# Softmax attention on one core: the second pair of heads taken in halves, one late group shared by two engines, and the order of the work read from a table

## The chip, the core and the metric

The kernel runs on one core of a Trainium2 chip. Five engines work side by side, each through its own list of instructions in order: TensorE (PE) multiplies matrices, VectorE (DVE) and ScalarE (ACT) work element by element, GpSimd (POOL) converts types here, and SyncE (SP) issues most of the transfers. They wait for each other by semaphores. The metric is the time of one execution on the device, in microseconds (us); below, a time without a unit is in us from the start of the profiled span.

## The reference

```python
def reference(q, k, v):                      # each 8 x 8 x 512 x 64, float32
    scale = 1.0 / np.sqrt(q.shape[-1])
    scores = np.einsum('bhqd,bhkd->bhqk', q, k) * scale
    scores = scores - scores.max(axis=-1, keepdims=True)
    attn = np.exp(scores)
    attn = attn / attn.sum(axis=-1, keepdims=True)
    return np.einsum('bhqk,bhkd->bhqd', attn, v).astype(np.float32)
```

That is 64 independent heads, each with 512 queries and 512 keys of 64 numbers, and 512 x 512 exponentials per head. The kernel leaves the subtraction of the maximum out and uses one constant shift instead; the division by the sum takes it out again.

## The kernel before

Two heads, a and b, make a *pair*; there are 32 pairs, 0 to 31. The 512 keys of a head are cut into 4 chunks of 128. The scores of one chunk of one head (128 keys by 512 queries) are a *block*, written a0 to a3 and b0 to b3, and two blocks are a *group*: one PSUM tile `st` of 128 x 1024 float32. There are 128 groups, `m` = 0 to 127; the last is worked in two halves of 256 queries, numbered 127 and 128. Three `st` tiles exist, so the scores of group m use the tile that group m-3 held.

What each pair goes through:

- **Load** (SP, `load`): k, q and v, 256 KB each, seven buffers of each.
- **Round to fp16** (`cast`): POOL writes k and q into `qkp` and v into `vp`. For pair 1, VectorE rounds half of q (line 523) and POOL the other half (line 524).
- **Turn** (PE, `transposes`, line 558): 8 transposes per pair into a PSUM bank `tp`; VectorE copies the result to `tqk` (line 571; for pair 1 in two copies, first k and then q of both heads, line 565). In `tqk` head a lies on partitions 0 to 63 and head b on 64 to 127.
- **Scores** (PE, line 598): two matmuls of 64 x 128 by 64 x 512 per group.
- **Exponential**: ScalarE makes one ACTIVATE of a whole group (line 602) into `pt`. 16 of the groups (`ON_DVE`) go to VectorE instead: `raise_` (line 625) reads the scores out of PSUM, which frees the `st` tile, and five passes (lines 642 to 665) make two fp16 factors, `pe` and `pd`, whose values are both fed to PE.
- **Values** (PE, line 704): for each head 4 *units* of 128 queries; each is 4 matmuls, and one more for every block that VectorE made. Seven units share a PSUM bank `o`. When a bank is full, VectorE takes the reciprocals of the sums (`rec`, line 671) and multiplies (`mul`, line 676) into a ring buffer, from which SP stores. `tp` and `o` share two banks, so a new `o` waits for the `mul` two banks before it.
- **The last head** has code of its own: `last_values` in four parts, the last two after the halves 127 and 128, and then `finish`: reciprocal, multiply, store.

The order of all this is written by `Plan`, a planner that steps through time with built-in costs (lines 18 to 425) and returns a list of steps; each step then records instructions on its engine. The order is fixed: an engine that waits holds back what is listed after it. Pair 0 is worked by its own code, `first_pair`, and its last group (m = 3) is the first that the planner's steps give to ScalarE.

Of the kernel before, what the change touches and what calls it, by code (L numbers as in the profile page):

```python
# [17 lines left out]
class Plan:  # L18

    SLOT, EXP, EXP_DONE, EXP_FIXED = 216, 853, 181, 64  # L20
    INTO, OUT_OF = 96, 96
    TRANSPOSE, V_UNIT = 222, 128
    TO_ACT, TO_DVE, TO_PE = 220, 210, 60

    COPY, NORM, RAISE = (601, 690), (50, 133), (1132, 1215)
    RECIPROCAL = 115
    SCALE, PRODUCT, EXTRA = 333, 600, 29
    COPY_1 = (400, 190)
    NORM_COLUMN, PASS_DONE = 67, 115
    PASSES = (SCALE, SCALE, PRODUCT, SCALE, PRODUCT)  # L30
    BITS = 2
    NEEDS = (None, None, 0, 2, 3)
    FIRST_EXP = 5000
    STEP = 5
    CALM, KEEN = 9000, 4
    FIRST_UNIT = 4
    KNOWN, OVER = (13, 15, 18, 20, 22, 24, 27, 42, 50, 61, 69, 97), 6
    ON_DVE = (5, 10, 16, 25, 28, 39, 44, 54, 63, 66, 74, 81, 91, 96, 103, 116)

    LATE_NORM, LATE_COPY, HURRY, SOON, BACKLOG = 700, 1500, 800, 160, 600  # L40
    LATE_MUL, WAIT = 400, 200
    SLACK, AHEAD = 0, 2

    CAST, CAST_PORT, CAST_DONE, TO_POOL = 557, 475, 130, 150
    SCALE_PORT, PRODUCT_PORT, GAP, REACH = 271, 537, 20, 5
    FIRST_LAND, LOAD, STORE, LATENCY, ISSUE = 5200, 752, 376, 2300, 470
    QUEUED, URGENT = 3500, 16
    PAIRED, STORE_ISSUE = 18, 520
    RAW, QK16, NV, NU = 7, 5, 12, 112
    PAIR, DUEK, DUEV, DUEL, PRE = 3300, 3550, 6000, 5000, 0  # L50

    def __init__(self, groups, pairs, first):
        self.groups, self.pairs = groups, pairs
        self.pe, self.act, self.dve = 7000, self.FIRST_EXP, 6300
        self.pool, self.port, self.dma = 4600, 4600, self.FIRST_LAND
        self.m, self.tiled = first, True
        self.read = []
        self.exps = {}
        for m in range(first):
            self.act += self.EXP + self.EXP_FIXED  # L60
            self.exps[m] = self.act + self.EXP_DONE
            self.read.append(self.exps[m])
        self.tq = {0: 5800}
        self.transposed = {0: 5800}
        self.next_t = 1
        self.part_t = 0
        self.banks = [5100, 5800]
        self.todo = [(g, h) for g in range(pairs) for h in range(2)]
        self.last = self.todo.pop()
        self.last_part = 0  # L70
        self.head = None
        self.units = self.FIRST_UNIT
        self.member = {b: m for m, grp in enumerate(groups) for b in grp}
        self.ready = []
        self.passes = []
        self.passed = {}
        self.raised = set()
        self.steps = []
        self.busy_dve = 0
        self.order, self.paired = [], 0  # L80

        late = {grp[0][0] for m, grp in enumerate(groups) if m in self.ON_DVE}
        due = []
        for g in range(pairs):
            scores = 5000 + self.PAIR * g
            if g:
                due += [(scores - self.DUEK, g, "k"), (scores - self.DUEK + 10, g, "q")]
            due.append((scores + self.DUEV + (self.DUEL if g in late else 0), g, "v"))
        self.due = sorted(due)
        self.uncast = list(self.due)  # L90
        self.casts = []
        self.landed, self.cast_done = {}, {}
        self.first_loads = [(g, n) for _, g, n in self.due if g < self.RAW]
        self.first_loads += [(self.RAW, "k"), (self.RAW, "q")]
        for x in self.first_loads:
            self.dma += self.LOAD
            self.landed[x] = self.dma
        self.loads, self.stores, self.stored = [], [], []
        self.sp = 1650 + 470 * len(self.first_loads)

    def note(self, t, *what):
        self.steps.append((t, len(self.steps)) + what)

    def trigger(self, t):

        ops = self.ops
        if not ops or ops[-1][1] <= t - 300:  # L110
            return 1, None
        n = len(ops) - 1
        while (
            n > 0
            and len(ops) - n < self.REACH
            and not ops[n][2]
            and ops[n][0] - ops[n - 1][1] <= self.GAP
        ):
            n -= 1
        if n > 0 and ops[n][0] - ops[n - 1][1] <= self.GAP:  # L120
            n -= 1
        return len(ops) - n, ops[n][1]

    def emit(self, t, back, after):
        _, g, n = self.uncast.pop(0)
        shared = (g, n) == (1, "q")
        self.note(t, "cast", g, n, back if t > self.CALM else 0)
        if not shared:
            self.casts.append((g, n, t if after is None else after + self.TO_POOL))
# [3 lines left out]
    def fits(self, t, soon=0):  # L133
        if not self.uncast:
            return False
# [763 lines left out]
```

## Time and profile before

| | us |
|---|---|
| median of 3 runs (113.44 to 113.83) | 113.63 |
| the profiled execution, whole | 113.92 |
| its span, first to last instruction | 112.1 |
| ScalarE busy in the span | 105.5 |
| TensorE busy | 103.2 |
| VectorE busy | 100.8 |
| GpSimd busy | 65.9 |

The profile is of one execution. The terms of a sum are differences inside that execution; it took 0.29 more than the median, and that offset, like the 1.8 outside the span, is carried along unchanged. In the rows, a line such as "9.21 1.02 ACT L602 ACTIVATE pt<-st" says: starts at 9.21, lasts 1.02, on ScalarE, from line 602, writes `pt` and reads `st`; in brackets stand the engine's idle time before it and what ended it. Where "x5" ends a row, five instructions in a row are merged, and the duration runs from the first start to the last end.

### The profile page before, as it was taken

The page shows a single profiled execution, that of the slowest core. Times are in us where ns is not written, and L with a number is a line of the kernel's source. Part 1 is how long each engine was busy: PE and PEld are TensorE (multiplying, and loading weights), DVE is VectorE, ACT ScalarE, POOL GpSimd, SP SyncE. Part 2 cuts the span into 40 slices and gives each one's busy share as a digit, 9 for nine tenths or more (in the row PEclk, how much of TensorE's full clock was granted, in tenths as well). Part 3 has the DMA queues.
Part 4 walks back from the last instruction along what each step waited for, and adds up shares of the span by engine and source line. Part 5 has one row for each costly group of instructions (what it writes and reads, how often), then busy time and mean ns, then how long its engine had stood idle before and what let it go on. Part 6 is the DMA issues. An engine that isn't in the chain of part 4 may idle for free.

```text
span 112.1 us, 4408 instructions
## 1 busy us (share of the span) xinstructions
PE 103.2 (92%) x1728; PEld 69.4 (62%) x1728; DVE 100.8 (90%) x227; ACT 105.5 (94%) x118; POOL 65.9 (59%) x127
## 2 busy tenths in 40 slices
PE   7978889999799998999989999899999999999980
PEld 7634555766367766658647767577557577675660
DVE  1647999999999999999999999999999999997390
ACT  4599999999999999999999999999999999999970
POOL 2147768549756886495594786876784855600000
PEclk9999999999999999999999999999999999999997
DMA  3999999999999999999999999999999974142354
GB/s 106 276 359 353 345 350 347 355 336 349 345 347 336 341 346 343 354 364 375 370 358 382 350 355 377 354 372 362 343 366 305 349 245 143 52 141 99 97 167 161
DMA packets 35093, 33.84 MB, mean 302 GB/s; under 512 B 2304, under 2 KB 35072, under 8 KB 35072
## 3 DMA queue, kind: packets, MB, share of 16 engines
q1 hardware_dynamic: 34496, 33.04, 90.4%
q10 hardware_dynamic: 576, 0.52, 1.4%
q8 instruction: 13, 0.21, 0.8%
q14 instruction: 8, 0.07, 0.2%
HBM read 25.17 MB, written 8.39 MB: 299 GB/s over the span
## 4 chain that ended last, share of the span: by engine, by line
DVE 39%; PE 24%; DMA 15%; issue 8%; POOL 7%; SPq 3%; ACT 2%; POOLq 0%; ACTq 0%
PE o L704 13%; DMA v<-in_v_dram 10%; PE st L598 8%; DVE pd L625 8%; DVE tqk L571 7%; DVE ring L676 7%; DMA q<-in_q_dram 5%; DVE m L659 4%; POOL qkp L525 4%; DVE pd L665 4%; POOL vp L515 3%; PE tp L558 2%; SPq L509 2%; DVE m L642 2%; DVE pe L651 2%
## 5 line engine op out<-in xcount | busy, mean ns | idle before, releaser
L602 ACT ACTIVATE pt<-st 128x1024 f16<-128x1024 f32 (+1 forms) x110 | 100.3, 1144 | 0.2 <-PE st L598 0.2
L704 PEld LDWEIGHTS <-pt 128*128 128x128 f16 x880 | 38.8, 98 | 12.1 <-issue 10.2
L704 PE MATMUL o<-vp,pt 128*128 128x65 f16 x880 | 45.3, 194 | 0.4 <-POOL vp L515 0.2
L598 PE MATMUL st<-tqk 64*128 64x512 f16 (+1 forms) x250 | 41.7, 380 | 2.6 <-ACT pt L602 1.4
L525 POOL CAST qkp<-k 128x512 f16<-128x512 f32 x31 | 22.2, 717 | 11.3 <-DVE rc L671 5.3
L525 POOL CAST qkp<-q 128x512 f16<-128x512 f32 x30 | 21.7, 725 | 9.0 <-DVE rc L671 5.3
L515 POOL CAST vp<-v 128x512 f16<-128x512 f32 x32 | 21.4, 679 | 9.2 <-PE st L598 2.4
L676 DVE TENSOR_TENSOR ring<-o,rc 128x448 f32<-128x448 f32 (+2 forms) x37 | 22.3, 606 | 0.4
L704 PE MATMUL o<-vp,pe 128*128 128x65 f16 x128 | 21.8, 194 | 0.0
L704 PE MATMUL o<-vp,pd 128*128 128x65 f16 x128 | 21.7, 192 | 0.0
L558 PE MATMUL tp<-ident,qkp 128*128 128x128 f16 x248 | 19.6, 220 | 1.6 <-DVE tqk L571 0.8
L558 PEld LDWEIGHTS <-qkp 128*128 128x128 f16 x248 | 14.4, 97 | 9.9 <-issue 4.6
L571 DVE COPY tqk<-tp 128x1024 f16<-128x1024 f16 x30 | 20.3, 683 | 0.0
L625 DVE TENSOR_SCALAR pd<-st 128x1024 uint16<-128x1024 f32 x16 | 19.5, 1216 | 0.7 <-PE st L598 0.7
L598 PEld LDWEIGHTS <-tqk 64*128 64x128 f16 x250 | 10.7, 93 | 11.8 <-issue 4.6
L704 PEld LDWEIGHTS <-pe 128*128 128x128 f16 x128 | 12.5, 98 | 3.4 <-issue 3.3
L704 PEld LDWEIGHTS <-pd 128*128 128x128 f16 x128 | 12.5, 98 | 0.0
L659 DVE TENSOR_TENSOR m<-m 128x1024 f16<-128x1024 f16 x16 | 11.0, 685 | 0.0
L665 DVE TENSOR_TENSOR pd<-pd,m 128x1024 f16<-128x1024 f16 x16 | 10.9, 684 | 0.0
L671 DVE RECIPROCAL rc<-o 128x7 f32<-128x7 f32 (+2 forms) x37 | 7.4, 199 | 2.6 <-PE o L704 2.4
L661 DVE TENSOR_SCALAR m<-m 128x1024 f16<-128x1024 f16 x16 | 6.7, 418 | 0.1
L651 DVE TENSOR_SCALAR pe<-pd 128x1024 uint16<-128x1024 uint16 x16 | 6.6, 411 | 0.0
(51 smaller groups left out, 34.9 us busy)
## 6 DMA issues: line engine op xcount, KB each, us to landing
v<-in_v_dram SPq DMA_DIRECT2D x32, 256.0 KB, 5.8
k<-in_k_dram SPq DMA_DIRECT2D x31, 256.0 KB, 5.8
q<-in_q_dram SPq DMA_DIRECT2D x31, 256.0 KB, 5.9
out_dram<-ring SPq DMA_DIRECT2D x18, 256.0 KB, 5.5
out_dram<-ring SPq DMA_DIRECT2D x25, 128.0 KB, 2.2
k<-in_k_dram ACTq DMA_DIRECT2D x2, 128.0 KB, 2.8
q<-in_q_dram SPq DMA_DIRECT2D x2, 128.0 KB, 2.6
out_dram<-ring ACTq DMA_DIRECT2D x2, 128.0 KB, 1.9
```

Of the source, the lines that this page charges most:

```text
L515: return nc.gpsimd.tensor_copy(out=vps[g % NV][:, :, :, 0:D], in_=raw[g]["v"][:, :, :, :])
L525: return nc.gpsimd.tensor_copy(out=dst, in_=src[:, :, :, :])
L558: reads[g] = nc.tensor.transpose(tps[g][:, n, i, :], qkp[g][:, n, i, :], ident)
L571: nc.vector.tensor_copy(out=tqk[g][:, :, :], in_=tps.pop(g).rearrange("p n i c -> p n (i c)"))
L598: nc.tensor.matmul(st[:, x, cols], kc, qc[:, cols], start=True, stop=True)
L602: ins = nc.scalar.activation(out=pt[:, :, cols], in_=st[:, :, cols], func=EXP, scale=scale, bias=SHIFT)
L625: nc.vector.tensor_scalar(out=r["pd"][:, :, :], in0=r["st"][:, :, :], scalar1=BITS, scalar2=BIAS, op0=AluOp.mult, op1=AluOp.add,)
L651: ins = nc.vector.tensor_scalar(out=r["pe"][:, :, :], in0=u[:, :, :], scalar1=0x7C00, scalar2=None, op0=AluOp.bitwise_and,)
L659: ins = nc.vector.tensor_tensor(out=m16, in0=m16, in1=m16, op=AluOp.mult)
L665: ins = nc.vector.tensor_tensor(out=u16, in0=u16, in1=m16, op=AluOp.mult)
L676: nc.vector.tensor_tensor(out=ring[:, u % NU : u % NU + n, :], in0=o[:, x : x + n, 0:D], in1=rcs.pop(u)[:, 0:n].broadcast_to([P, n, D]), o ...
L704: nc.tensor.matmul(os[u // 7][:, u % 7, :], part[:, y * P : (y + 1) * P], vps[g % NV][:, h, c, :], start=(n == 0), stop=(n == len(parts) - 1),
```

## The change

Five things change; the arithmetic of the result does not.

1. **The order** is no longer planned: `Order` holds it as text, one letter per step (S scores, T transposes, V a unit of values, K a cast, C a copy, R a raise, N and M a bank's reciprocals and multiply, and so on). Counts of every kind of step stay what they were, apart from pair 1. The groups on VectorE are again 16, but other ones.
2. **Pair 1** is loaded as four transfers of 128 KB (k and q of head a, then of head b) instead of two of 256 KB, rounded head by head (k on POOL, q on VectorE), turned head by head and copied head by head. Its groups are a0a1, a2b0, a3b1, b2b3 where they were a0b0, a1b1, a2b2, a3b3, so the first needs head a alone.
3. **The last pair**: a0b0, a1b1, a2a3, b2b3 where it was a0a1, a2a3, b0b1, b2b3.
4. **Group 120**, the last of the 16, is shared: ScalarE takes its first block, VectorE raises the second alone. Before, the last of the 16 was group 116, wholly on VectorE.
5. A cast's dependence on VectorE is counted along one list, `trail`; the fp16 tiles of a raised group are taken at the raise.

```diff
+class Order:
+
+    ON_DVE = (5, 11, 15, 26, 31, 38, 47, 55, 59, 71, 81, 84, 96, 103, 108, 120)
+    SPLIT = (120,)
+    PAIR_1 = "a0a1 a2b0 a3b1 b2b3"
+    LAST_PAIR = "a0b0 a1b1 a2a3 b2b3"
...
+        "KSDKTDCTKSCKSSRKTTSKCVVVaSNScVSKMTdTbSCKVVRKSVTKSeTSCVKSfKRSTGKTVSKCVSkTNgSKMTSCKVVhSGVV"
...
+            if g == 1 and name in "kq":
+                halves.append((load_tile(g, name), source(src, g)))
+                if len(halves) == 2:
+                    for h in range(2):
+                        for t, rows in halves:
+                            nc.sync.dma_start(out=t[:, h], in_=rows[:, h])
+                continue
...
-        if (g, name) == (1, "q"):
-            nc.vector.tensor_copy(out=dst[:, :, 0:2], in_=src[:, :, 0:2])
-            return nc.gpsimd.tensor_copy(out=dst[:, :, 2:4], in_=src[:, :, 2:4])
+        dst, src = rounded(g, name), raw[g][name]
+        if g == 1:
+            h = "kq".index(name)
+            return nc.gpsimd.tensor_copy(out=rounded(1, "k")[:, h], in_=raw[1]["k"][:, h])
...
+    def cast_queries(h):
+        dve(nc.vector.tensor_copy(out=rounded(1, "q")[:, h], in_=raw[1]["q"][:, h]))
...
+    def head_transposes(h, bank):
+
+
+        cols = slice(0, 64 + 64 * h)
+        t = ps_x.tile([P, 2, NI, P], FP16, tag=f"x{bank ^ h}", name=f"tp_1_{h}")
+        for n in (1, 0):
+            for i in range(NI):
+                reads[1] = nc.tensor.transpose(t[cols, n, i, :], qkp[1][:, n, i, cols], ident)
+        flips.append(t)
...
+            h = len(copied)
+            rows = slice(64 * h, 64 * h + 64)
+            copied.append(
+                dve(
+                    nc.vector.tensor_copy(
+                        out=tqk[1][rows, :, :], in_=flips[h][rows].rearrange("p n i c -> p n (i c)")
+                    )
+                )
+            )
...
+        own = 0 if on_dve and m not in Order.SPLIT else 1 if on_dve else 2
...
+            if x < own:
+                blocks[(g, c, h)] = [pt[:, x, :]]
+        if own == 0:
             return
         ins = nc.scalar.activation(
-            out=pt[:, :, cols], in_=st[:, :, cols], func=EXP, scale=scale, bias=SHIFT
-        )
...
+            out=pt[:, 0:own, cols], in_=st[:, 0:own, cols], func=EXP, scale=scale, bias=SHIFT
+        )
...
-                out=r["pd"][:, :, :],
-                in0=r["st"][:, :, :],
+                out=r["pd"][:, own:2, :],
+                in0=r["st"][:, own:2, :],
```

**VectorE at pair 1, before.** Its list from the end of pair 0 on (`qkp` are the rounded k and q, `tqk` the turned ones, `tp_1_0` the turned k and `tp_1_1` the turned q, `pd_5` the first raise):

```order
L835 COPY qt_0_169<-tp_qb_180 128x256 [waits PE_49]
L523 CAST qkp_1_275<-q32_1_110 128x2x2x64 [waits DMAHW5_49]
L565 COPY tqk_1_284<-tp_1_0_285 128x512 [waits PE_49]
L565 COPY tqk_1_284<-tp_1_1_293 128x512 [waits PE_49]
L625 TENSOR_SCALAR pd_5_307<-st_5_305 128x1024 [waits PE_49]
L571 COPY tqk_2_317<-tp_2_0_318 128x1024 [waits PE_49]
```

**The same place after.** Here `tp_1_0` and `tp_1_1` are head a and head b:

```order
L563 COPY qt_0_171<-tp_qb_182 128x256 [waits PE_49]
L241 CAST qkp_1_277<-q32_1_109 128x4x64 [waits DMAHW5_49]
L241 CAST qkp_1_277<-q32_1_109 128x4x64 [waits DMAHW7_49]
L281 COPY tqk_1_286<-tp_1_0_287 64x1024 [waits PE_49]
L281 COPY tqk_1_286<-tp_1_1_298 64x1024 [waits PE_49]
L350 TENSOR_SCALAR pd_5_325<-st_5_316 128x1024 [waits PE_49]
L288 COPY tqk_2_328<-tp_2_329 128x1024 [waits PE_49]
```

Both casts of q stand ahead of both copies, and the second waits for the fourth transfer.

**VectorE at the last raise, before.** `rc` and `ring` are the reciprocals and the multiply of a bank of units (the numbers behind `rc` count units), `m` the passes' working tile:

```order
L671 RECIPROCAL rc_210_2696<-o_30_2649 128x7 [waits PE_49]
L676 TENSOR_TENSOR ring_85<-o_30_2649,rc_210_2696 128x448 [waits DMAHW6_49,DVE_49]
L625 TENSOR_SCALAR pd_116_2701<-st_116_2699 128x1024 [waits PE_49]
L571 COPY tqk_31_2721<-tp_31_0_2722 128x1024 [waits PE_49]
L642 TENSOR_SCALAR m_116_2758<-pd_116_2701 128x1024 [waits DVE_49]
L651 TENSOR_SCALAR pe_116_2700<-pd_116_2701 128x1024
L659 TENSOR_TENSOR m_116_2758<-m_116_2758 128x1024 [waits DVE_49]
L671 RECIPROCAL rc_217_2793<-o_31_2685 128x7 [waits PE_49]
```

**The same place after:**

```order
L399 RECIPROCAL rc_217_2773<-o_31_2713 128x7 [waits PE_49]
L350 TENSOR_SCALAR pd_120_2782<-st_120_2761 128x512 [waits Activation_49]
L404 TENSOR_TENSOR ring_85<-o_31_2713,rc_217_2773 128x448 [waits DMAHW4_49,DVE_49]
L399 RECIPROCAL rc_224_2818<-o_32_2775 128x7 [waits PE_49]
L393 TENSOR_TENSOR pd_108_2504<-pd_108_2504,m_108_2645 128x1024
L404 TENSOR_TENSOR ring_85<-o_32_2775,rc_224_2818 128x448 [waits DMAHW5_49,DMAHW1_49,DVE_49]
L399 RECIPROCAL rc_231_2866<-o_33_2827 128x7 [waits PE_49]
L370 TENSOR_SCALAR m_120_2873<-pd_120_2782 128x512
L404 TENSOR_TENSOR ring_85<-o_33_2827,rc_231_2866 128x448 [waits DMAHW4_49,DVE_49]
```

The raise waited for PE; now it waits for ScalarE, which reads the other half of the same tile, and the multiply of bank `o_31` and the last pass of group 108 are listed behind it.

**TensorE at the scores that take the raised tile, before** (`st_119` takes the tile of group 116; the other names are values of pair 25 and scores of pair 30):

```order
L704 MATMUL o_31_2685<-vp1_87,pd_103_2396 128x65
L598 LDWEIGHTS tqk_29_2459
L598 MATMUL st_119_2753<-tqk_29_2459 128x512 [waits DVE_49]
L598 MATMUL st_119_2753<-tqk_29_2459 128x512
L598 LDWEIGHTS tqk_30_2614
L598 MATMUL st_120_2760<-tqk_30_2614 128x512 [waits Activation_49]
```

**and after** (`st_122` and `st_123` are scores of pair 30, `o_33` the next bank of values):

```order
L316 MATMUL st_122_2813<-tqk_30_2550 128x512
L316 LDWEIGHTS tqk_30_2550
L316 MATMUL st_123_2821<-tqk_30_2550 128x512 [waits DVE_49]
L316 MATMUL st_123_2821<-tqk_30_2550 128x512
L432 LDWEIGHTS pt_116_2668
L432 MATMUL o_33_2827<-vp5_91,pt_116_2668 128x65 [waits DVE_49]
```

(In both, the weight load before a tile's second matmul is left out, as it only repeats.) The scores of group 123 wait for the raise of group 120, whose tile they take, and the bank `o_33` waits for the multiply of `o_31`. Behind these stand, in this order: 20 matmuls of values of pair 29, 10 of group 108's pair (its `pd` is one of the factors), the scores of groups 124 and 125, 34 and 4 matmuls of values, the scores of 126 and 127, 28 matmuls of values (20 of them with the factors of group 120), the scores of 128, 16 of head a of the last pair, and the last head.

More of the change, by code (lines that the diff above doesn't have):

```diff
@@ L1 @@
 import math
+import re
 from contextlib import ExitStack
@@ L477 @@
     raw = {}
+    halves, flips, copied = [], [], []
     qkp = {}
@@ L866 @@
         }
-        for what, *args in steps:
+        for what, *args in order.steps():
             do[what](*args)
```

531 lines of the change are left out of this document (118 added, 413 removed), and 13 rows, old and new, of tables (CASTS, HEADS, LOADS).

## Prediction

> **What bounds the kernel now.** I read the page first, for the busy shares:
>
> ```profile
> span 112.1 us, 4408 instructions
> PE 103.2 (92%) x1728; PEld 69.4 (62%) x1728; DVE 100.8 (90%) x227; ACT 105.5 (94%) x118; POOL 65.9 (59%) x127
> ACT  4599999999999999999999999999999999999970
> ```
>
> Three engines lie within 5% of each other, so shares don't decide; what decides is which engine never waits. The chain of waits wanders (VectorE, TensorE, GpSimd, transfers), which says that most of them are just in time. ScalarE's own instructions in order of time, and then its groups by shape, settle it:
>
> ```profile
> 5.20 0.60 ACT L801 ACTIVATE pt<-st_0a 128x512 f16<-128x512 f32 x1 [0.43 <-PE st_0a L794]
> 5.69 0.59 ACT L801 ACTIVATE pt<-st_0b 128x512 f16<-128x512 f32 x1
> 6.17 1.95 ACT L801 ACTIVATE pt<-st 128x1024 f16<-128x1024 f32 x2
> 7.98 1.06 ACT L602 ACTIVATE pt<-st 128x1024 f16<-128x1024 f32 x1
> 9.21 99.28 ACT L602 ACTIVATE pt<-st 128x1024 f16<-128x1024 f32 x109 [0.18 <-PE st L598]
> ```
>
> ```profile
> L602 ACT ACTIVATE pt<-st 128x1024 f16<-128x1024 f32 x108 | 99.4, 1153 | 0.2 <-PE st L598 0.2
> L602 ACT ACTIVATE pt<-st 128x512 f16<-128x512 f32 x2 | 1.1, 616 | 0.0
> ```
>
> The exponentials overlap, so their mean of 1153 ns is no price; the distance of their ends is. The first half ends at 5.20+0.60 = 5.80 and the second at 5.69+0.59 = 6.28: 0.48 for a half. Group 4 ends at 9.21+1.02 = 10.23 (its row stands below) and the last at 9.21+99.28 = 108.49; between lie 106 whole groups and two halves, so a whole one costs (98.26 - 0.96)/106 = 0.918. Groups 1 and 2, with nothing to wait for, end together at 8.12, 1.84 after group 0: 0.92 each. So from 10.23 to 108.49 ScalarE ran at the price it has undisturbed: nothing is to be gained there unless it does fewer exponentials. Its only lost time is ahead of group 4: group 3 ended at 7.98+1.06 = 9.04, group 4 could have ended at 9.96 and ended at 10.23, 0.27 later. After the last exponential the span goes on for 3.6.
>
> The Trainium skill (ScalarE: Activation LUTs, What ACT_TABLE_LOAD costs) gives an ACTIVATE with immediate scale and bias 186 ns + 0.833 ns per element, less 93 ns of overlap: an estimate of 0.95 for a group and 0.52 for a half. The rows have 0.918 and 0.48, so the measurement decides; by the page the first term below would be 0.04 larger.
>
> How much room is there before ScalarE waits? An exponential that had to wait lasts 1.02 from start to end:
>
> ```profile
> L602 ACT ACTIVATE pt<-st x9: 1024/1057/1110, 99.1 to 106.5; 128x1024 f16<-128x1024 f32 x9
> ```
>
> One that lasts longer stood ready beside the one before it. Near the end the shortest took 1.024: that group's scores came with no room at all. A schedule that is a little later there makes ScalarE wait, with all the rest behind it.
>
> **First term: the shared group.** Both lists have 16 groups on VectorE, but the last now leaves its first block to ScalarE: one half more, **+0.48**, on the engine that sets the time. Nothing covers it. What it saves (VectorE half a raise and five half passes, PE four matmuls of values) lies on engines that ScalarE doesn't wait for.
>
> **Second term: the start.** Pair 1 before:
>
> ```profile
> 6.65 0.62 POOL L525 CAST qkp<-k 128x512 f16<-128x512 f32 x1 [2.98 <-DMA k<-in_k_dram]
> 7.32 0.94 PE L558 MATMUL tp<-ident,qkp 128*128 128x128 f16 x8 [0.44 <-POOL qkp L525]
> 7.37 0.29 DVE L523 CAST qkp<-q 128x256 f16<-128x256 f32 x1 [1.15 <-DMA q<-in_q_dram]
> 7.40 0.52 POOL L524 CAST qkp<-q 128x256 f16<-128x256 f32 x1
> 7.76 0.97 DVE L565 COPY tqk<-tp 128x512 f16<-128x512 f16 x2
> 8.78 0.82 PE L598 MATMUL st<-tqk 64*128 64x512 f16 x6 [0.52 <-DVE tqk L565]
> 9.21 1.02 ACT L602 ACTIVATE pt<-st 128x1024 f16<-128x1024 f32 x1 [0.18 <-PE st L598]
> 9.43 1.23 DVE L625 TENSOR_SCALAR pd<-st 128x1024 uint16<-128x1024 f32 x1 [0.70 <-PE st L598]
> 10.57 0.68 DVE L571 COPY tqk<-tp 128x1024 f16<-128x1024 f16 x1
> ```
>
> k lands at about 6.6 and q at 7.35, so 0.75 per 256 KB. The same bytes in four parts land at about 6.22, 6.6, 6.98 and 7.37. VectorE rounds q of head a by 6.9 (0.29), the transposes take 0.6 after it (7.66 to 8.26 before) and end at 7.5. The copy can't start then: the second cast of q stands ahead of it and ends at 7.66. The copy's 64 x 1024 isn't in the trace; its bounds are 0.42 to 0.49 (the 512-element copies) and 0.68 (1024 elements), and I take 0.68, since the rows differ by elements per partition. It ends at 8.3. Group 4 is now two blocks of one head: its matmuls use the same rows of PE and follow each other, 0.21 more than two heads, by these rows of the chain and of the timeline:
>
> ```profile
> 102.98 0.60 PE st L598 x2
> ```
>
> ```profile
> 97.60 0.39 PE L598 MATMUL st<-tqk 64*128 64x512 f16 x2
> ```
>
> From the first matmul to the exponential it was 9.21-8.78 = 0.43; so 8.33+0.43+0.21 = 8.97, 0.24 earlier: **-0.24**. At best all 0.27 come back; at worst none, if the small transfers land late. Head b's copy ends at 9.0, so the raise of group 5 stays at 9.5 (9.43 before) and pair 2's copy with it. Two more transfers on SP cost it two issues, under cover of a queue that is full. The rest of the order table I cost at nothing: steps of the same kinds and number; its cover is the room ScalarE has in front of each group.
>
> **Third term: what waits for group 120.** Prices of one step, from the chain, where each piece runs to the start of the next:
>
> ```profile
> 13.76 1.13 DVE pd L625
> 20.97 0.11 DVE rc L671
> 21.37 0.53 DVE ring L676
> 21.91 0.60 DVE pd L665
> 33.77 1.40 PE o L704 x40
> 35.17 0.54 PE st L598 x4
> ```
>
> A matmul of values is 1.40/40 = 0.035. A half raise isn't in the trace: between 0.56 (half of 1.13) and 1.13, nearer the half, and I take 0.60 with 0.69 to its own end (the multiplies of 256 and 448 elements, 0.42 and 0.62, differ by 1.0 ns per element; 1.23 less 512 of these). Let Z be the end of the half exponential of 120. Without waits the last one ends at Z + 6 x 0.918 + 0.98 = Z+6.49. VectorE reaches this raise early (what is listed ahead of it waits only for values that PE lists before the scores of 120, and these come two groups before ScalarE needs them) and is held there until Z, since it waits for ScalarE. It ends at Z+0.7; PE stands at the scores of 123 and starts them at Z+0.75. The multiply behind the raise ends at Z+1.25, so bank `o_33` starts at Z+1.3; the last pass of 108 (after a reciprocal) ends at Z+1.95 and is in time. 30 matmuls: Z+2.38, the scores of 124. They were needed by: end of exponential 123 (Z+2.75) + 0.918 - 1.02 - 0.43 = Z+2.22. **+0.16.** Scores of 124 and 125, then 38 matmuls, put the scores of 126 at Z+4.2, and 126 is of one head: its exponential starts at Z+4.85 and ends at Z+5.87; from 124 on it would have been Z+5.67. **+0.20.** The last exponential ends at Z+6.85. Bounds of this term: 0 (VectorE not held) and 0.8 (the raise at the whole price of 1.13 holds PE 0.5 longer).
>
> **Fourth term: the last steps.** Now:
>
> ```profile
> 107.49 0.68 PE L704 MATMUL o<-vp,pt 128*128 128x65 f16 x16
> 108.01 0.84 PE L720 MATMUL o_last<-vp,pt 128*128 128x65 f16 x16
> 108.43 0.42 DVE L676 TENSOR_TENSOR ring<-o,rc 128x256 f32<-128x256 f32 x1
> 108.89 0.18 DVE L733 RECIPROCAL rc_last<-o_last 128x4 f32<-128x4 f32 x1
> 109.55 0.33 SPq L740 DMA_DIRECT2D out_dram<-obl x1
> ```
>
> The last head's reciprocal starts 0.40 after the last exponential. Head a of the last pair now needs group 126 (its a2a3) instead of 125, so its 16 matmuls start about when 128's scores are done, Z+6.05, and end at Z+6.65; its reciprocal and multiply (0.22, 0.42) end at Z+7.5 and stand ahead of `rc_last`: Z+7.53 instead of 6.85+0.40 = 7.25. **+0.28**, with bounds of 0 and 0.4.
>
> **Sum:** 0.48 - 0.24 + 0.36 + 0.28 = +0.88. On the profiled 113.92 that is 114.80; on the median, 113.63, it is 114.51.
>
> **Rivals.**
>
> *The wait at group 120 is covered.* If PE gets through its values somewhat faster, or the raise isn't held, terms three and four nearly vanish: 0.48 - 0.24 = +0.24, 113.9. For it: the list keeps most of this work early enough to miss by 0.2 only. Against: shortest exponential of 1.024, no room. The Trainium skill (PSUM — Partial Sum Buffer, Specifications (TRN2)) says that ScalarE and VectorE read PSUM in parallel at full bandwidth if their banks differ; by that rule the raise could run beside the half exponential. In this list it waits for it, whatever the banks allow.
>
> *The price of ScalarE isn't a floor (faster).*
>
> ```profile
> 7.07 1.04 ACT L801 ACTIVATE pt<-st 128x1024 f16<-128x1024 f32 x1
> ```
>
>  Starts follow each other by 0.91, as group 2's and group 3's (7.98) do, where ends do by 0.918; were the difference a wait for scores, up to 0.01 x 106 = 1.1 would be left in the order, and a better table would take it out: 113.63 + 0.24 - 1.1 = 112.8. It decides from a price below 0.912 per group on. Against it: the two undisturbed groups at the start cost 0.92.
>
> *The small transfers land late.* Pair 1 gains nothing and the sum is +1.12: 114.75.
>
> *The new table makes ScalarE wait in mid-run.* 15 other groups sit on VectorE, each holding one of three tiles. If ten of them cost 0.1, +1.0: 115.5. For it: the room above. Against: the list before has it nowhere after 10.23.
>
> **How the numbers follow.** Mine 45%, covered wait 25%, late transfers 10%, waits in mid-run 12%, floor not a floor 8%. The likeliest is 114.5, its own range 114.1 to 114.9. The range reaches down to the covered case and up half way to the mid-run waits: 113.8 to 115.2. A measurement of this kernel can tell about 0.3%, 0.34, from no change: below 113.29 lies only the floor rival, 8%; within lie some two thirds of the covered case, 17%; the rest, 75%, is slower.
>
> **What would show it.** Right: group 4's exponential at about 9.0; distance of ends still 0.918 up to group 120; VectorE idle ahead of a 128x512 raise, released by ScalarE; idle time of ScalarE at the end, released by PE; the last reciprocal more than 0.4 after the last exponential. Wrong: ScalarE's groups closer than 0.912, or VectorE's raise of 120 well before the half exponential ends.

## The result, and the profile after

The changed kernel takes **115.27 us** (median of 4 runs, 115.11 to 115.47), and the kernel before, on the same chip, 113.73 (113.44 to 114.05). The ratio is **1.0136**, with a 95% interval of 1.0103 to 1.0168: slower by 1.54. The forecast was 114.5, 113.8 to 115.2.

The profiled executions are 115.25 and 113.92, their spans 113.48 and 112.10; the difference of the spans, 1.38, is what the rows below divide up. (The medians are 1.54 apart; the profiled execution of the kernel before took 0.19 more than its median.) First the busy shares of the changed kernel:

```profile
PE 106.5 (94%) x1732; PEld 70.3 (62%) x1732; DVE 102.1 (90%) x228; ACT 106.3 (94%) x119; POOL 63.0 (56%) x127
```

The shares say as little as before; PE's busy time even rose by 3.3 with four matmuls more. ScalarE's instructions in order of time say more (line 529 is pair 0, line 321 the rest):

```profile
6.13 1.95 ACT L529 ACTIVATE pt<-st 128x1024 f16<-128x1024 f32 x2
7.93 6.78 ACT L321 ACTIVATE pt<-st 128x1024 f16<-128x1024 f32 x7
14.92 94.69 ACT L321 ACTIVATE pt<-st 128x1024 f16<-128x1024 f32 x104 [0.20 <-PE st L316]
```

Before, the first group of pair 1 (group 4) was late; now its exponential follows the one before. But there are two new losses. The seven ending at 7.93+6.78 = 14.71 follow one that ended at 8.08: 6.63, where seven back to back take 7 x 0.917 = 6.42. By the single ends in the trace, 0.226 is lost ahead of group 7, the last of pair 1. And 0.311 is lost ahead of group 12, the first of pair 3, which starts at 14.92. From there on the ends are 0.917 apart again (0.915 to 0.918 for 100 of the groups), up to the end of the kernel:

```profile
104.20 1.24 ACT L321 ACTIVATE pt<-st 128x1024 f16<-128x1024 f32 x1
105.55 1.94 ACT L321 ACTIVATE pt<-st 128x1024 f16<-128x1024 f32 x2
107.61 1.51 ACT L321 ACTIVATE pt<-st 128x1024 f16<-128x1024 f32 x2
```

The first row is group 123, ending at 105.44. Groups 124 and 125 end together at 107.49, 2.05 later instead of 1.83, and 126 with the first half after it at 109.12, 1.63 later instead of 1.41: 0.22 lost ahead of 124 and 0.23 ahead of 126.

| part of the span | before | after | difference |
|---|---|---|---|
| end of the first two half exponentials | 6.28 | 6.24 | -0.04 |
| waits of ScalarE up to group 12 | 0.335 | 0.537 | +0.20 |
| small waits and rounding in between | 0.02 | 0.04 | +0.02 |
| the half exponential of group 120 | none | 0.490 | +0.49 |
| waits ahead of 124 and 126 | none | 0.446 | +0.45 |
| last exponential to the landing of the last store | 2.77 | 2.80 | +0.03 |
| that landing to the end of the span | 0.84 | 1.06 | +0.22 |
| sum | | | +1.37 |

**The start.** The rows around pairs 1 to 3 in the changed kernel:

```profile
5.08 0.38 PE L522 MATMUL st<-qt,kt 64*128 64x512 f16 x2
7.47 1.41 DVE L281 COPY tqk<-tp 64x1024 f16<-64x1024 f16 x2 [0.63 <-PE tp L272]
9.31 0.61 POOL L226 CAST qkp<-q 128x512 f16<-128x512 f32 x1
9.47 0.91 PE L263 MATMUL tp<-ident,qkp 128*128 128x128 f16 x8
10.31 0.60 PE L316 MATMUL st<-tqk 64*128 64x512 f16 x2
10.78 0.61 POOL L226 CAST qkp<-k 128x512 f16<-128x512 f32 x1
11.09 0.58 DVE L370 TENSOR_SCALAR m<-pd 128x1024 uint16<-128x1024 uint16 x1
11.53 0.61 POOL L226 CAST qkp<-q 128x512 f16<-128x512 f32 x1
11.71 0.98 DVE L387 TENSOR_TENSOR m<-m 128x1024 f16<-128x1024 f16 x1
12.61 0.34 DVE L404 TENSOR_TENSOR ring<-o,rc 128x192 f32<-128x192 f32 x1
13.10 0.61 PE L263 MATMUL tp<-ident,qkp 128*128 128x128 f16 x8 [0.61 <-DVE ring L404]
13.74 0.69 DVE L288 COPY tqk<-tp 128x1024 f16<-128x1024 f16 x1
```

The four halves land at 5.42, 5.76, 6.14 and 6.51, far earlier than I had put them (6.22 to 7.37), and the copies of pair 1 start at 7.47 (7.76 before). But pair 2's k and q land at 8.54 and 9.26, against 8.09 and 8.85. The cast of q (9.31) and with it the transposes (9.47 to 10.38) are late, and the scores of group 7, which need neither, stand behind those transposes: 10.31. From the landing of that q to the end of group 7's exponential it takes 2.715 here, and 2.718 and 2.715 in the two other executions of the new table in which group 7 waited (experiments 3 and 9): the landing sets this wait.

Pair 3 is late for another reason. Its copy (13.74) follows its transposes (13.10), and these need a bank that the multiply of the first units (line 404) frees; that multiply now stands behind the product pass of line 387, at 12.61. And this pass took 0.98, beside the cast of pair 3's q on GpSimd (11.53 to 12.14), as the pass of line 370 took 0.58 beside that of k; with no cast beside them these passes take 0.69 and 0.42 (experiments 5 and 10). In the kernel before:

```profile
10.72 0.62 POOL L525 CAST qkp<-k 128x512 f16<-128x512 f32 x1 [0.46 <-DVE pd L625]
11.56 0.72 POOL L525 CAST qkp<-q 128x512 f16<-128x512 f32 x1 [0.23 <-DVE rc L671]
11.73 0.35 DVE L676 TENSOR_TENSOR ring<-o,rc 128x192 f32<-128x192 f32 x1
12.49 0.67 DVE L659 TENSOR_TENSOR m<-m 128x1024 f16<-128x1024 f16 x1
13.09 0.68 DVE L571 COPY tqk<-tp 128x1024 f16<-128x1024 f16 x1
```

There both casts of pair 3 waited for VectorE, the product pass took 0.67, and one other pass was held up beside a cast (line 651, 0.57). In the new table (`3k 3q`, without a number) they wait for their loads alone, and start 0.05 after these land. From the copy of pair 2 to that of pair 3 it took 2.52 before, with three passes between, and 3.24 now, with four.

**The end.** Around the raise of group 120:

```profile
102.72 0.69 DVE L350 TENSOR_SCALAR pd<-st 128x512 uint16<-128x512 f32 x1 [0.93 <-ACT pt L321]
103.33 0.61 DVE L404 TENSOR_TENSOR ring<-o,rc 128x448 f32<-128x448 f32 x1
103.47 0.39 PE L316 MATMUL st<-tqk 64*128 64x512 f16 x2 [0.29 <-DVE pd L350]
103.99 0.80 PE L432 MATMUL o<-vp,pt 128*128 128x65 f16 x20
105.06 0.61 PE L316 MATMUL st<-tqk 64*128 64x512 f16 x4
106.91 0.60 PE L316 MATMUL st<-tqk 64*128 64x512 f16 x4
109.48 0.18 DVE L399 RECIPROCAL rc<-o 128x4 f32<-128x4 f32 x1
109.70 0.42 DVE L404 TENSOR_TENSOR ring<-o,rc 128x256 f32<-128x256 f32 x1
110.04 0.17 DVE L461 RECIPROCAL rc_last<-o_last 128x4 f32<-128x4 f32 x1
```

VectorE stood 0.93 for ScalarE with the raise at its head; PE then waited for the raise (103.47) and for the multiply behind it (103.99), and the scores of 124 and 126 came at 105.06 and 106.91.

**After the last landing.** Instructions of SyncE at the kernel's last line, from the last store's landing on, in the kernel before and then in the changed one (last line 894 and 622; the window opens at 111.26 and at 112.41):

```profile
L894 SPq EVENT_SEMAPHORE  x2: 17/22/28, 111.3 to 111.6; - x2
```

```profile
L622 SPq EVENT_SEMAPHORE  x6: 17/28/1305, 111.1 to 112.9; - x6
```

SyncE checks the transfers' semaphores one after the other. In the changed kernel it stood in one of these checks for 1.3 when the store landed, and four more came after, at 112.467, 112.531, 112.593 and 112.652; in the kernel before one came, at 111.276. (The last of each row belongs to the steps that end every execution.) Three more at 0.062 are 0.19 of the 0.22.

### The profile page after: what moved, and what is told of

Same layout as the page of the kernel before. It is cut to its first block, busy times and chain, and to the rows that moved or that the text cites. A ratio compares the mean times of both kernels' runs of the same rounds, so it can differ in the third digit from the quotient of the medians.

```text
span 113.5 us, 4391 instructions
## 1 busy us (share of the span) xinstructions
PE 106.5 (94%) x1732; PEld 70.3 (62%) x1732; DVE 102.1 (90%) x228; ACT 106.3 (94%) x119; POOL 63.0 (56%) x127
## 4 chain that ended last, share of the span: by engine, by line
PE 54%; DVE 25%; ACT 12%; issue 4%; DMA 1%
PE o L432 22%; PE st L316 18%; ACT pt L321 12%; PE tp L263 8%; DVE pd L350 5%; DVE tqk L288 5%; DVE ring L404 5%; DVE m L387 3%; PE st_0a L479 3%; DVE pd L393 2%; DMA out_dram<-ring 1%; DVE m L370 1%; DVE rc L399 1%; DVE m L389 1%; DVE pe L379 1%
## 5 line engine op out<-in xcount | busy, mean ns | idle before, releaser
L432 PE MATMUL o<-vp,pt 128*128 128x65 f16 x884 | 48.3, 195 | 0.2
L316 PE MATMUL st<-tqk 64*128 64x512 f16 (+1 forms) x250 | 44.7, 382 | 1.6 <-ACT pt L321 0.5
L226 POOL CAST qkp<-k 128x512 f16<-128x512 f32 x30 | 21.0, 700 | 16.9 <-DVE pd L393 5.1
L219 POOL CAST vp<-v 128x512 f16<-128x512 f32 x32 | 22.2, 701 | 10.4 <-DVE pd L393 5.4
L226 POOL CAST qkp<-q 128x512 f16<-128x512 f32 x30 | 19.1, 647 | 5.9 <-DVE m L389 2.3
L350 DVE TENSOR_SCALAR pd<-st 128x1024 uint16<-128x1024 f32 (+1 forms) x16 | 18.9, 1180 | 1.5 <-ACT pt L321 0.9
L387 DVE TENSOR_TENSOR m<-m 128x1024 f16<-128x1024 f16 (+1 forms) x16 | 11.1, 698 | 0.0
L393 DVE TENSOR_TENSOR pd<-pd,m 128x1024 f16<-128x1024 f16 (+1 forms) x16 | 10.6, 664 | 0.1
L389 DVE TENSOR_SCALAR m<-m 128x1024 f16<-128x1024 f16 (+1 forms) x16 | 6.6, 412 | 0.1
L370 DVE TENSOR_SCALAR m<-pd 128x1024 uint16<-128x1024 uint16 (+1 forms) x16 | 6.6, 415 | 0.0
```

What stands on the lines that cost most here:

```text
L219: return nc.gpsimd.tensor_copy(out=vps[g % NV][:, :, :, 0:D], in_=raw[g]["v"][:, :, :, :])
L226: return nc.gpsimd.tensor_copy(out=dst, in_=src[:, :, :, :])
L316: nc.tensor.matmul(st[:, x, cols], kc, qc[:, cols], start=True, stop=True)
L350: nc.vector.tensor_scalar(out=r["pd"][:, own:2, :], in0=r["st"][:, own:2, :], scalar1=BITS, scalar2=BIAS, op0=AluOp.mult, op1=AluOp.add,)
L387: ins = nc.vector.tensor_tensor(out=m16, in0=m16, in1=m16, op=AluOp.mult)
L393: ins = nc.vector.tensor_tensor(out=u16, in0=u16, in1=m16, op=AluOp.mult)
```

## The experiments

Each was timed beside the kernel before on its own chip. The ratio is to that; the changed kernel has 1.0136. The transfers of the first pairs land some tenths earlier or later from one execution to the next, and with them the waits up to group 12; in ten executions with halves, pair 2's q landed between 8.3 and 9.8. The intervals of all versions of the changed kernel overlap its own, so no time by itself sets two of them apart. So the small steps are judged by the waits that the trace shows, and the ratio is shown beside them. A wait can also go because ScalarE comes later to it, having waited before; so the time at which a group ends is given where that matters.

**1. The whole of group 120 on VectorE**, as it was for the last group before.

```diff
-    SPLIT = (120,)
+    SPLIT = ()
```

> The changed kernel with group 120 wholly on VectorE again. Theory (sharing costs half an exponential and holds VectorE's list until ScalarE has read its half): 0.48 of work and the two waits of 0.22 and 0.23 ahead of groups 124 and 126 go, 115.27 - 0.93 = 114.3; the raise of 120 waits for TensorE and starts about 2 earlier. Rival (the waits at the end come from how many matmuls of values stand between the scores, whoever raises): only the work goes, 114.8, and ScalarE still waits ahead of 124 and 126. Second rival: five whole passes make the factors of 120 late and a wait of some 0.3 appears ahead of group 128.

Measured: 115.73 (115.51 to 116.49), 1.0178 [1.0102, 1.0253]: not faster, though ScalarE does half an exponential less. In its trace:

```profile
101.59 1.17 DVE L350 TENSOR_SCALAR pd<-st 128x1024 uint16<-128x1024 f32 x1
107.05 0.69 DVE L393 TENSOR_TENSOR pd<-pd,m 128x1024 f16<-128x1024 f16 x1
107.80 0.20 PE L432 MATMUL o<-vp,pd 128*128 128x65 f16 x1 [0.70 <-DVE pd L393]
109.25 0.60 ACT L321 ACTIVATE pt<-st 128x512 f16<-128x512 f32 x1 [0.68 <-PE st L316]
```

The raise isn't held any more. But its passes are twice as long, the last ends at 107.74, PE waits 0.70 for it, and the scores of the last half stand behind those values: 0.783 lost ahead of it, besides 0.27 and 0.234 earlier. By these waits, 1.29 in all against 0.45 and the half's 0.49, sharing the group costs less in this order than raising it whole; that the half exponential is a cost is not thereby wrong, but it isn't to be had back by this edit.

**2. The multiply that frees the bank for `o_33` ahead of the raise** (parts of two lines of the table).

```diff
-MVSnSwNVRVw"
-"VVVMVVSNw
+MVSnSwNVMRVw"
+"VVVVVSNw
```

> The changed kernel with one step moved: the multiply of units 217 to 223 is listed ahead of the raise of group 120 instead of behind it. Theory: bank o_33 is free before the raise ends, so TensorE gets from the scores of 123 to those of 124 by 0.35 sooner; the wait ahead of 124 (0.22) goes and that ahead of 126 falls from 0.23 to about 0.1: 115.27 - 0.35 = 114.9. Rival (number of matmuls): no change, 115.3.

Measured: 115.08 (114.81 to 115.44, 10 runs), 1.0119 [1.0087, 1.0150]. VectorE's idle time ahead of the raise falls from 0.93 to 0.27, since the multiply fills it:

```profile
101.59 0.62 DVE L404 TENSOR_TENSOR ring<-o,rc 128x448 f32<-128x448 f32 x1
102.48 0.69 DVE L350 TENSOR_SCALAR pd<-st 128x512 uint16<-128x512 f32 x1 [0.27 <-ACT pt L321]
104.61 0.61 PE L316 MATMUL st<-tqk 64*128 64x512 f16 x4
106.46 0.60 PE L316 MATMUL st<-tqk 64*128 64x512 f16 x4
```

The wait ahead of 124 is 0.008 instead of 0.219, and from the start of the raise to the scores of 124 it takes 2.13 instead of 2.34: this wait is the multiply's place behind a held raise. The wait ahead of 126 stays, 0.230. So the two waits, which I had put down to one cause, have two. From the scores of 124 to those of 126 PE takes 1.85 in both kernels (104.61 to 106.46, 105.06 to 106.91), ScalarE's two exponentials 1.83, and 126 is of one head, whose two matmuls follow each other: 0.02 and the 0.21 of the prediction add up to the 0.23, which is a reckoning and not a test.

**3. Group 120 wholly on ScalarE** (15 groups on VectorE; its raise and its five passes leave the table too, which the lines below do not show).

```diff
-    ON_DVE = (5, 11, 15, 26, 31, 38, 47, 55, 59, 71, 81, 84, 96, 103, 108, 120)
-    SPLIT = (120,)
+    ON_DVE = (5, 11, 15, 26, 31, 38, 47, 55, 59, 71, 81, 84, 96, 103, 108)
+    SPLIT = ()
```

> The changed kernel with group 120 wholly on ScalarE, no raise and no passes for it (15 groups on VectorE). Theory: 0.918 - 0.48 = 0.44 more of work, 0.45 of waits less: about 115.27, the same as the shared group. Rival (waits come from the values): 115.7, or 115.6 with eight matmuls of values less.

Measured: 115.24 (114.96 to 116.42), 1.0142 [1.0057, 1.0228]. In its trace there is no wait at all at the end:

```profile
101.35 9.49 ACT L321 ACTIVATE pt<-st 128x1024 f16<-128x1024 f32 x11
```

So the waits ahead of 124 and 126 come from group 120's work on VectorE and in PE's list. Half an exponential more (0.43) for 0.446 of waits less is even, and as far as four runs tell the two kernels take the same. The profiled execution is the longest of the four, 116.42, by the start, which the edit doesn't touch: pair 2's q landed at 9.78, and groups 7, 8 and 12 lost 0.834, 0.400 and 0.622.

**4. The scores of 126 earlier too**, on top of steps 2 and 7 (below): they move ahead of four of the eight units listed between, 18 matmuls, about twice what the expectation says.

```diff
-wcVVVwdVNSeSM
+wcSVVVwdVNeSM
```

> As the run before, and the scores of group 126 listed two units of values earlier (8 or 10 matmuls, some 0.35 to 0.5). Theory: the wait of 0.23 ahead of 126 goes too and none takes its place, 114.6; then from group 119's end to the last exponential nothing but ScalarE's own 0.49 + 6 x 0.917 + 0.98 is left. Rival (group 126 waits for something else than TensorE's queue, such as its tile or pair 31's copy): no change against the run before.

Measured: 115.40 (115.21 to 115.91), 1.0111 [1.0044, 1.0177]. The wait ahead of 126 is gone and a larger one stands ahead of the last half, 0.503:

```profile
106.57 0.60 PE L316 MATMUL st<-tqk 64*128 64x512 f16 x2
107.78 0.39 PE L316 MATMUL st<-tqk 64*128 64x256 f16 x2
109.09 0.39 PE L316 MATMUL st<-tqk 64*128 64x256 f16 x2
109.52 0.60 ACT L321 ACTIVATE pt<-st 128x512 f16<-128x512 f32 x1 [0.40 <-PE st L316]
```

TensorE does not wait for group 120's last pass here, which ends at 108.26, ahead of the first values that use it. It has more to do. The scores of 126 and of the first half, of different heads, took 0.60 together (106.91 in the changed kernel); apart they take 0.60 and 0.39. From the scores of 124 to those of the last half it is 3.80 here (105.29 to 109.09), 3.38 in the changed kernel (105.06 to 108.44). So the move itself costs about 0.4 of TensorE's time, and the end has no room for it. A move that keeps the two side by side was not tried.

**5. Pair 1 in two transfers of 256 KB again**, all else as changed.

```diff
-                        for t, rows in halves:
-                            nc.sync.dma_start(out=t[:, h], in_=rows[:, h])
+                        t, rows = halves[h]
+                        nc.sync.dma_start(out=t[:, :, :, :], in_=rows)
```

> The changed kernel with pair 1's k and q loaded in two transfers of 256 KB, as before; rounding, turning and copying stay head by head. Theory (the four small transfers land pair 1 about 0.85 earlier but pair 2 0.45 later, and two transfers more shift the semaphore of the last store, so that SP checks three more after it landed): pair 1 lands at 6.6 and 7.35 again, ScalarE waits about 0.3 ahead of group 4, pair 2 lands at 8.1 and 8.85 and the wait of 0.23 ahead of group 7 goes; from the last landing to the end it takes 0.84 instead of 1.07. Sum about 115.27 + 0.3 - 0.23 - 0.2 = 115.1. Rival (group 7 waits because its two blocks are of one head and its scores stand behind pair 2's transposes, whatever the transfers): group 7 still waits 0.2 or more after group 4's wait is counted, 115.35.

Measured: 115.17 (114.93 to 116.06), 1.0103 [1.0034, 1.0171]; the profiled execution is the longest. k and q land at 7.36 and 8.12 (the last half at 6.51 in the changed kernel), and group 4 waits:

```profile
10.32 2.86 ACT L321 ACTIVATE pt<-st 128x1024 f16<-128x1024 f32 x3 [1.28 <-PE st L316]
```

That is 1.388 lost; groups 7 and 12, to which ScalarE comes that much later, lose 0 and 0.064, and SyncE's last checks take 0.84 from the last landing, not 1.06. In this execution the two landed 0.77 later than in the kernel before, and the other three, 0.7 to 1.1 shorter, were not traced. The halves bring forward what they are for; in the median that gain doesn't show.

**6. The four transfers alone, in the kernel before.** The diff is the loop of the change's second part, put into `before`.

> The kernel before with one thing done: pair 1's k and q are loaded in four transfers of 128 KB; all else as it was. Theory: pair 1 lands at 5.4 to 6.5 instead of 6.6 and 7.35 and pair 2 at 8.5 and 9.25 instead of 8.1 and 8.85; group 4's wait of 0.27 goes, but the scores of group 7 stand behind pair 2's transposes and wait about 0.2 more; the last store's semaphore adds 0.2 after its landing. Sum: between 0 and +0.2, 113.7 to 113.95. Rival (small transfers cost nothing later): 0.27 faster, 113.45.

Measured: 114.36 (113.93 to 114.81, 10 runs) against 113.95 (13 runs), 1.0021 [0.9987, 1.0055]: no gain. The halves land at 5.11 to 6.33, and group 4's wait of 0.288 is gone. Group 7 waits 0.345 instead:

```profile
9.55 0.62 POOL L523 CAST vp<-v 128x512 f16<-128x512 f32 x1 [0.41 <-DMA v<-in_v_dram]
10.22 0.41 PE L712 MATMUL o<-vp,pt 128*128 128x65 f16 x8 [0.30 <-POOL vp L523]
11.00 1.02 ACT L610 ACTIVATE pt<-st 128x1024 f16<-128x1024 f32 x1 [0.24 <-PE st L606]
```

In the old order its scores stand behind the first values of pair 0, and these wait for v, whose place in the queue is behind pairs 1 and 2. Before, group 7's exponential ended at 12.12, here at 12.02, by as much earlier as the very first one: a second limit stood right behind the one that was removed. Six more waits of 0.03 to 0.22 follow up to 43, 0.52 in all, which neither kernel had; what paced each of them was not settled. And the end costs 1.06.

**7. The multiply of the first units ahead of the product pass** (M and c exchanged).

```diff
-aSNScVSKMTdTb
+aSNSMVSKcTdTb
```

> The changed kernel with two steps of VectorE exchanged after the first raise: the multiply of the first bank (units 4 to 6) stands ahead of the first product pass of group 5 instead of behind it. Theory (the transposes of pair 3 wait for this multiply to free their bank, the copy of pair 3 follows, and ScalarE waits 0.31 for group 12): that wait goes, 115.27 - 0.3 = 115.0, and the transposes of pair 3 start at about 12.2 instead of 13.1. Rival (the transposes wait for the cast of pair 3, as GpSimd is late by the transfers): they start no earlier than 12.2 either way but group 12's wait stays above 0.2, 115.2.

Measured: 115.43 (115.00 to 115.58), 1.0135 [1.0051, 1.0220]. The multiply stands at 12.11, and group 12's wait falls from 0.311 to 0.061:

```profile
5.18 0.64 PE L522 MATMUL st<-qt,kt 64*128 64x512 f16 x2
12.11 0.36 DVE L404 TENSOR_TENSOR ring<-o,rc 128x192 f32<-128x192 f32 x1
12.39 0.68 DVE L387 TENSOR_TENSOR m<-m 128x1024 f16<-128x1024 f16 x1
13.78 0.68 DVE L288 COPY tqk<-tp 128x1024 f16<-128x1024 f16 x1
```

But pair 3's copy starts at 13.78 and group 12 ends at 15.98, where it was 13.74 and 15.95: nothing came earlier. ScalarE came to group 12 0.28 later, mainly since group 4 had lost 0.331, and so waited less.

Nor does the multiply's place shorten VectorE's way from the copy of pair 2 to that of pair 3. It takes 2.80 and 2.81 where the multiply stands as in the changed kernel and no cast runs beside the passes (experiments 5 and 10), and 2.81 with the multiply moved (here and experiment 4). With a cast beside the product pass it is 3.09 to 3.24 (experiments 1 and 2 and the changed kernel; in experiment 3, where the transposes came late too, 4.04), and with one beside another pass 2.95 to 3.07 (experiments 8, 9 and 11). In the four executions with a cast beside it the product pass started while the cast ran and ended 0.54 after the cast's end. So group 12's wait in the changed kernel is these passes, held up beside the casts, in a list that had room for less. No run holds the casts back as the kernel before did.

Group 4's loss isn't the landing of the halves (5.85 and 6.21). In four executions with halves (experiments 7, 9, 10 and 11) it lost 0.30 to 0.33, in experiment 9 with halves landed at 5.09 to 6.42; in the other seven at most 0.024. In the four, TensorE's two matmuls of group 1's scores, at about 5.1, took 0.63 each instead of 0.38, at a granted clock of 1.00 in both, and pair 0's last copies on VectorE, ahead of the casts of pair 1's q, came 0.35 to 0.41 later, counted from the first exponential. Why TensorE took longer there is open.

**8. Pair 2 in halves too.**

```diff
-            if g == 1 and name in "kq":
+            if g in (1, 2) and name in "kq":
```

> The changed kernel with pair 2's k and q in four transfers of 128 KB too. Theory A (a transfer of 256 KB at the start lands late by its shape, small ones land as their bytes come): pair 2 lands at about 7.4 to 8.0 instead of 8.5 and 9.25, and group 7 no longer waits: 115.27 - 0.2 = 115.05. Theory B (bytes and the issue on SP set it): pair 2 lands no earlier than 8.2, group 7 still waits, and later loads move by another 0.4: 115.3 to 115.6.

Measured: 115.20 (115.11 to 115.64), 1.0120 [1.0061, 1.0179]. Pair 2 has landed at 8.41 (9.26), and group 7's wait is gone. Group 12 still loses 0.202, and 0.45 are lost at five places between 43 and 65, where the changed kernel loses 0.07. Such losses stand in experiments 4, 6 and 9 too, so they are not put down to this edit.

**9. Both multiplies moved** (steps 2 and 7 together).

> The changed kernel with both multiplies moved: that of units 217 to 223 ahead of the raise of 120, and that of the first bank ahead of the first product pass of group 5. Theory: the two gains add, 0.22 ahead of group 124 and 0.25 ahead of group 12, where the start's transfers land as in the changed kernel: 115.27 - 0.45 = 114.8. Rival (ScalarE gives back at the next group what it gains at one): 115.1 as with the late multiply alone.

Measured: 115.15 (114.74 to 116.21, 10 runs), 1.0112 [1.0073, 1.0152]. Groups 12 and 124 lose 0.045 and 0.006. The profiled execution had pair 2's q landing at 9.81; group 4 lost 0.328 and group 7 0.44, so ScalarE came to group 12 0.56 later than in the changed kernel, and group 12 ended at 16.24 instead of 15.95. So the trace shows the gain ahead of 124 alone, and not that two gains add.

**10. The scores of group 7 ahead of pair 2's transposes.**

```diff
-CKSSRKTTSKCVVV
+CKSSRKSTTKCVVV
```

> The changed kernel with the scores of group 7 listed ahead of pair 2's transposes. Theory (group 7 waits 0.23 because it stands behind transposes whose q lands late): its wait goes; the transposes come 0.3 to 0.4 later and pair 2's copy with them, so group 8 waits instead, 0.1 to 0.3, and the time stays within 0.2 of 115.27. Rival (the wait is the copy of head b or the tile of group 4): group 7 waits as before.

Measured: 115.76 (115.45 to 116.01), 1.0134 [1.0069, 1.0199]. Group 7 waits no more, but group 8 does:

```profile
10.49 0.59 PE L316 MATMUL st<-tqk 64*128 64x512 f16 x2 [0.39 <-ACT pt L321]
11.01 0.62 PE L263 MATMUL tp<-ident,qkp 128*128 128x128 f16 x8
12.85 3.83 ACT L321 ACTIVATE pt<-st 128x1024 f16<-128x1024 f32 x4 [0.58 <-PE st L316]
```

The scores of 7 wait for a free tile, the transposes of pair 2 stand behind them although its q landed at 8.32, and group 8, the first of pair 2, loses 0.683. (Group 4 had lost 0.303, as said under 7, and that tile came free so much later.) The transposes were in the right place; where group 7 waited, it was for a q that came too late for that place.

**11. Two stores fewer**, on top of step 4: the heads of two late pairs leave in one transfer of 256 KB each (`W`, one step) instead of two of 128 KB (`w`, two).

> The kernel with three moves, and two pairs of heads (24 and 26) stored by one transfer each instead of two, so that the kernel has as many transfers as the one before. Theory (the last store's semaphore is picked by the count of transfers, and SP checks its semaphores one after another): from the last landing to the end 0.84 instead of 1.06, 114.4. Rival (it is the shape of the loads that matters): 1.06 again.

Measured: 115.19 (114.69 to 115.77, 10 runs), 1.0089 [1.0055, 1.0124], against 115.40 and 1.0111 without it. From the last landing to the end it is 0.83 instead of 1.07, and the wait for that landing is again the last:

```profile
L622 SPq EVENT_SEMAPHORE  x2: 17/22/28, 112.8 to 113.1; - x2
```

So the end follows the number of transfers. Three pairs show it: 0.84 and 1.06 for before and before with two transfers more, 1.06 and 0.84 for after and after with two fewer loads, 1.07 and 0.83 here; 144 transfers have the short end, 146 the long one, and experiment 8, with 148, has 1.08. No version that was run beats the kernel before.

## Why the prediction was right and wrong

**Right: ScalarE sets the time, at a price that is a floor.** 0.917 a group and 0.49 a half, with the new table as with the old; the rival of a price below 0.912 is out. "First term: the shared group", forecast +0.48, measured +0.49.

**Right in place, low in size: "Third term: what waits for group 120".** Forecast 0.16 ahead of 124 and 0.20 ahead of 126, measured 0.219 and 0.227, with VectorE idle ahead of the raise, released by ScalarE, as named. Experiment 3 shows that both hang on group 120, experiment 2 that the first is the multiply behind the raise. That both have one cause is wrong: the second stays when the first is gone. The rival of a covered wait falls.

**Wrong: "Second term: the start", forecast -0.24, measured +0.20.** The term ends with group 4, and there its best case came true: in the profiled execution all of the 0.288 is gone. (In four of the eleven executions with halves group 4 lost 0.30 to 0.33 all the same, by TensorE's pace in pair 0; see experiment 7.) What failed stands behind it.

First, the next limit. With ScalarE early, group 7 hangs on the landing of pair 2's q: 9.26, 9.81 (experiment 9) and 9.78 (3) cost 0.226, 0.44 and 0.834, and each time group 7 ends 2.715 to 2.718 after the landing. At 9.29 (experiment 4), with the first exponentials 0.31 later, it cost nothing, nor did landings from 8.41 to 8.93. "Two more transfers on SP cost it two issues, under cover of a queue that is full" says nothing of what lands behind them. Whether the two transfers themselves make pair 2 late is not shown: with halves its q landed between 8.3 and 9.8, with whole transfers at 8.85 and 9.59. The trace of before had a sign of the next limit: by the single ends group 7 lost 0.047 there, where the prediction, from a mean over 106 groups, read nothing after 10.23.

Second, "The rest of the order table I cost at nothing; steps of the same kinds and number". The number was the same, the places and the waits were not. Between the copies of pairs 2 and 3 VectorE had four passes instead of three (0.28 more, 2.80 for 2.52), and the casts of pair 3 no longer waited for VectorE, so that two of the passes ran beside them (0.44 more). Together they cost 0.311 ahead of group 12, which in all eleven executions of the new table ended 2.19 to 2.21 after pair 3's copy started. The rival of waits in mid-run had ten of 0.1; there was one of 0.3 near the start, and between it and the end 0.05 in all.

The times of landing were wrong by 0.8, to the other side, and so were those of the casts and copies that were built on them. The rival of late small transfers falls, though its sum of +1.12 comes nearer to the result than mine.

**Wrong: "Fourth term: the last steps", forecast +0.28, measured +0.03.** The order was as described, `rc_last` stands behind head a's reciprocal and multiply. But the term's own figures don't add up: from Z+6.65 the two take 0.22 and 0.42, which is Z+7.29, and I wrote Z+7.5. The 0.21 between has no row, and without it the term is about +0.07. In the rows head a's matmuls end at 109.44, and the three instructions start at 109.48, 109.70 and 110.04, 0.56 from the first to the third. And from the half exponential's end (Z = 102.69) the last exponential was 0.07 later than forecast. So `rc_last` came 0.43 after it, not 0.68.

**Missed: +0.22 after the last landing.** The forecast carried "what lies behind" unchanged. It changed because the number of transfers did.

Of the terms as measured, 0.49 + 0.45 + 0.20 + 0.22 are 1.36 of 1.38. The forecast's sum of 0.88 had two terms with a compensating error (the start too low by 0.44, the last steps too high by 0.25) and left one out.

What stays open: why the medians give back so little when a wait is taken out early. One profile for each version can't tell, since the landings, TensorE's pace in pair 0 and the casts that fall beside a pass differ from one execution to the next. Small waits between group 12 and the end, 0.43 to 0.65 in sum, stand in the traces of experiments 4, 6, 8 and 9, and 0.05 to 0.07 in those of the changed kernel and its other versions; what each waits for was not followed to its end.

## What to carry to other kernels

Where the bound engine runs back to back, cost a new order of the others by the work that each frees: look for the step that releases a bank or a tile, and ask what is now listed ahead of it, and what now runs beside it: a wait that the old order had may have kept two engines apart. Where a wait goes, follow the list on to the next thing that lands or is freed, before the gain is counted. Taking one wait out of an order without room moves it to the next tight place; the sum of such waits is not what is to be gained. And a wait that shrank proves no gain by itself: look whether the group behind it ended earlier.

## What the hardware showed that I had not expected

Four transfers of 128 KB land earlier than the same bytes in two of 256 KB, not only the first but also the last of them: 6.28 to 7.06 for the fourth half in eleven executions, 7.35 and 8.12 for the second whole one. The lead does not hold on to the next pair, whose q landed between 8.3 and 9.8 with halves ahead of it and at 8.85 and 9.59 without. The product pass (`m<-m`, 128 x 1024) is held up when it starts while a cast runs on GpSimd: over all thirteen traces the 32 that started 0.13 or more ahead of a cast's end all ended 0.54 after that end, up to 1.11 after their start; the other 166 took 0.67 to 0.69. The copies of 128 x 1024 out of PSUM were not held up, 0.64 to 0.69 with a cast or without. The end of a kernel isn't a constant: which of SyncE's checks is the last to wait decided 0.84 or 1.06 from the last landing to the end of the span, by two transfers more or less, 144 or 146.
